# Wider splits, one evacuation for two PSUM banks, and half-size cache chunks in a decode layer with GLA and dilated attention

## The chip, the cores and the metric

The kernel runs on one core of a Trainium2 chip. The metric is device time in microseconds (us) of one execution. In the profile PE is TensorE (matrix multiply), PEld its weight load, DVE VectorE, ACT ScalarE, POOL GpSimd, SP SyncE (which only issues DMAs here).

## What is computed

One layer of a hybrid decoder on 544 tokens, 512 of a new prompt and 32 sampled ones (8 sequences of 4 tokens) whose attention reads a cached window. The reference, cut to what matters here:

```python
def layer(x):                                    # x: 544 tokens x 2048
    h = rmsnorm(x)
    gq, gk, gv, gg, glr, aq, ak, av = split(h @ w_in)
    log_a = log_sigmoid(glr @ w_gk_up + b_gk) / 16
    gla_o = gla_chunked(gq, gk, gv, log_a, state)    # 4 heads, S_t = diag(a_t) S_{t-1} + k_t v_t
    # 8 heads, each query sees keys t - j*dil, j = 0..128, for dil = 1, 4, 16; sampled tokens read the cache
    att_o = combine([window_attention(aq, ak, av, cache, dil) for dil in (1, 4, 16)])
    y = concat(rmsnorm(gla_o) * silu(gg), rmsnorm(att_o))
    x = x + y @ w_out
    return x + square(relu(rmsnorm(x) @ w_up)) @ w_down
y = final_rmsnorm(layer(x))                      # also: new keys and values, GLA states
```

## The kernel before

Activations stand transposed, 128 features by 544 tokens a tile, and every large product is weights times such tiles in two column halves of 272. For precision each f32 factor is split into a high part (rounded to fp32r) and a low part (the remainder), and three products are summed: high by high, high by low, low by high.

The stages on TensorE, in order: the in-projection (`slot_main`, slots 6 to 95), the output projection (`wo`, slots 96 to 127), the MLP as units of 12 matmuls, a last block and the final norm. A slot is half of the contraction of one block of 128 output features: 8 weight tiles of 128x128, three products, two column halves, 48 matmuls. Two slots fill one pair of PSUM banks, one bank for each half of the tokens; `bank[0..3]` are two such pairs. The first 16 slots of `wo` (96 to 111) read the attention's output, the other 16 that of GLA.

Ahead of its slot, weights are loaded (`raw`, 512 KB) and split by `split_w`: ScalarE copies to the high part `wh`, VectorE subtracts to the low part `wl`. A slot's weights are split in two units of 128x512, each with one instruction for the high and one for the low part, in rings of four high and three low tiles, four units ahead (`AHEAD`). A block is evacuated by `evac_in`, `evac_att` and `evac_wo` (VectorE) with one instruction per bank, 128x272.

The attention and GLA run in the background of the in-projection: they are Python generators, and `bg`, called twice in a slot, steps them, so that their instructions are queued on each engine between those of the slots. The order on each engine is thus fixed when the program is built. `att_sample` is the attention of the sampled tokens: for each of two groups of four heads, key chunks and then value chunks are loaded by SyncE (`kvload`, `kv` tiles, a ring of `NKV`) and worked off by VectorE. A chunk holds `VE` positions of 320 columns each; a key position is one multiply-add (into two accumulators in turn), a value position one dot product; there are `NCH` key and `NCH` value chunks a group. One step of the generator is one chunk. `bg` steps `att_sample` under this condition, with a planner's clocks `clk` for each engine:

```python
while clk["V"] + 1000 < clk["P"] + TH_S and step(sgens):   # TH_S = 1000
    pass
```

and each call of a VectorE operation first lifts VectorE's clock to TensorE's (line 96 of the profile is this helper, which issues nearly every instruction):

```python
self.clk[self.key] = max(self.clk[self.key], self.clk["P"] - self.clk["lag"])
self.clk[self.key] += self.cost(name, a, k)
```

When the slots of the in-projection are through, `drain` steps what is left until the attention is finished, and only then `wo` is issued. Names in the rows: `kv` are cache chunks, `wh` and `wl` the parts of weights, `bank` PSUM, `b` any other tile, `ones` a matrix for sums over partitions, `AT`, `ktok`, `vtok`, `ST`, `dlS` tiles of GLA.

Of the kernel before, what the change touches and what calls it, by code (L numbers as in the profile page):

```python
# [16 lines left out]
HALF = 272  # L17
# [3 lines left out]
VE = 4  # L21
NCH = 32
NROW = 320
NKV = 3
# [20 lines left out]
NWH = 3  # L45
NWHI = 4
AHEAD = 4
NSLOT2 = 7
# [75 lines left out]
def _body(ctx, nc, tc, A):  # L124
# [6 lines left out]
    bank = [psum.tile([128, 512], F32, name=f"bank{i}") for i in range(8)]  # L131
    mbank = bank[:4]
# [14 lines left out]
    def alloc(dt=F32):  # L147
        cnt[0] += 1
        n = f"b{cnt[0]}"
        for free, p, tag, bufs in tiers:  # L150
            if free[0]:
                free[0] -= 1
                t = p.tile([128, NTOK], dt, name=n, tag=tag, bufs=bufs)
                home[id(t)] = (t, free)
                return t
        raise SystemExit(f"no slots at {slot[0]} {unit_no}")
# [70 lines left out]
    def low_parts():  # L227
        while todo:
            todo.pop(0)()

    def split_w(key, r, eng, lag=False):

        low_parts()
        h = whm[key] = pool.tile([128, 4, 128], R32, name="wh" + "_".join(map(str, key)), tag="wh", bufs=NWHI)
# [11 lines left out]
        if not lag:  # L246
            low_parts()

    def split_q(i, q):
        split_w((i, q), raws[i][:, 4 * q:4 * q + 4, :], V, True)  # L250
# [13 lines left out]

    def wops(i):
        return (lambda c: whm[i, c // 4][:, c % 4, :]), (lambda c: wlm[i, c // 4][:, c % 4, :])
# [158 lines left out]
    def evac_in(idx, pb):  # L425
        kind, h, _ = order[idx]
        t = alloc()
        sc = QSCALE if kind in ("q", "gq") else 1.0
        for hf in range(2):
            V.scalar_tensor_tensor(half(t, hf), pb[hf][:, :HALF], sc, half(r_bc, hf), op0=OP.mult, op1=OP.mult)  # L430
        B[kind, h] = t
        ready[kind, h] = slot[0]
        if kind in ("q", "k", "v"):
            j = "qkv".index(kind)
            S.activation(KVS[h // 4][:, j * 128 + (h % 4) * 32:j * 128 + (h % 4) * 32 + 32], t[:, SEQ:], AF.Copy)
        if kind in ("k", "v"):
            dst = A["kT" if kind == "k" else "vT"][h]
            defer(1, lambda: nc.sync.dma_start(dst, t))
# [551 lines left out]
    for c in range(14):  # L990
# [12 lines left out]
        if c == 13:  # L1003
            for k in range(c - 2, 16):
                xsquare(k)
            load()
# [5 lines left out]
    for n in range(3):  # L1012
        xmm(n, 14)
        xmm(n, 15)
        if n == 0:
            prep_to(2)
            V.tensor_add(ssA, ssA, ssB)
            rms_r(r_bc, [ssA], D, (b0, b1))
            rel(ssA, ssB, *sqt)
# [36 lines left out]
    def slot_main(i, pb, xs_, c0, first, last, evac=None, nbg=1, hs=(0, 1)):  # L1056
        begin()
        load_to(i + NRAW + 1)
        prep_to(uidx[i] + AHEAD)
        h, l = wops(i)  # L1060
        for q in range(2):
            clk["P"] = max(clk["P"], spl[i, q])
# [11 lines left out]
            if q == 0:  # L1074
                prep_to(uidx[i] + AHEAD + 1)
# [115 lines left out]
    def evac_att(nb):  # L1191
        def f(pb):
            for hf in range(2):
                V.tensor_add(half(xr[nb], hf), pb[hf][:, :HALF], half(xr[nb], hf))
        return f

    def evac_wo(nb):
        def f(pb):
            t = xr[nb]
            for hf in range(2):  # L1200
                V.tensor_add(half(t, hf), pb[hf][:, :HALF], half(t, hf))
# [57 lines left out]
    FIRST = uidx[len(W) - 1] + 2  # L1259
# [55 lines left out]
    def product(key, ops, k, blocks, ps, start, stop):  # L1315
        def mm_():
            n = len(blocks)
# [32 lines left out]
    ua = [bank[0], bank[1]]  # L1350
    ub, uc = [bank[2], bank[6]], [bank[3], bank[7]]
# [3 lines left out]
    def halfb(b):  # L1355
        return b[:, :HALF]
# [64 lines left out]
    def up_after(p, k):  # L1421
        a, b, c = ua[p % 2], ub[p % 2], uc[p % 2]
# [5 lines left out]
        def f():  # L1428
            if k == "P1":
# [73 lines left out]
    for p, k, q in useq:  # L1503
        bk, st_ = ubank[k]
        i = len(units)
        for quad_, kk in last_read.items():
            if kk == k:
                raw_last["u", p, *quad_] = i
        add_unit(Unit((k, p, q), up_prep(p, k, q),
                      product((k, p, q), XU, k, range(4 * q, 4 * q + 4), halfb(bk[p % 2]), st_ and q == 0,  # L1510
# [35 lines left out]
    def down_after(g, p, k):  # L1546
        ps = halfb(bank[4 * (p % 2) + dbank[k][0]])

        def f():
            if g == 0 and k == "P1":  # L1550
                acc[2 * p], acc[2 * p + 1] = alloc(), alloc()
# [48 lines left out]
    for g in range(7):  # L1600
        for p in range(8):
            for i in range(2):
                raw_seq.append((("d", g, p, i), A["wdn"][g, 2 * p + i]))
            for k in D_ORDER:
# [3 lines left out]
                if k == "P4":  # L1608
# [3 lines left out]
                         product((k, g, p), XD[g], k, range(4), halfb(bank[4 * (p % 2) + b_]), st_, True),  # L1612
# [46 lines left out]
    LB = [bank[i] for i in (0, 1, 2, 3)]  # L1659
# [71 lines left out]
    def split_last(key, r):  # L1731
# [6 lines left out]
        h = whm[key] = pool.tile([128, 4, 128], R32, name="wh" + "_".join(map(str, key)), tag="wh", bufs=NWHI)  # L1738
# [5 lines left out]
    for hf in range(2):  # L1744
        for nb in range(16):
            raw_seq.append((("l", hf, nb), A["wdn"][7, nb]))
            for q in range(2):
                raw_last["l", hf, nb] = len(units)

                def prep(hf=hf, nb=nb, q=q):  # L1750
                    split_last(("L", hf, nb, q), mraw["l", hf, nb][:, 4 * q:4 * q + 4, :])
                add_unit(Unit(("L", hf, nb, q), prep, last_mm(hf, nb, q), before=last_before(hf, nb, q),
                              after=(lambda hf=hf, nb=nb: evac_last(hf, nb, LB[nb % 4])) if q else None))
# [39 lines left out]
    assert not later  # L1793

# [165 lines left out]
```

## Time and profile before

| | |
|---|---|
| three runs | 2323.55, 2325.3, 2328.4 us, median 2325.3 |
| the profiled execution | 2323.29 us, of which the span of the trace is 2321.5 us |
| TensorE busy | 2277.4 us, 98% of the span |
| VectorE busy | 1963.5 us, 85% |
| ScalarE busy | 1115.3 us, 48% |
| GpSimd busy | 126.7 us, 5% |
| DMA | 473.43 MB, mean 204 GB/s |
| in-projection, output projection | to 730 us; 730 to 927 us |

A busy share is an average over the span. A row of a timeline gives the start, the duration, the engine, the line and the operation with what it writes and reads; several equal instructions in a row are one row with their count, and in brackets stands how long the engine was idle before it and what ended that.

### The profile page before, as it was taken

To read this page: it belongs to the slowest core of one execution; us is meant where nothing else is said; L and a number is where in the kernel's file an instruction comes from. 1 tells how busy PE (TensorE), PEld (TensorE's weight loads), DVE (VectorE), ACT (ScalarE), POOL (GpSimd) and SP (SyncE) were. 2 spreads that over 40 slices of the span, in tenths; PEclk is the share of its full clock that TensorE was granted. 3 is DMA by queue.
4 is the path that set the end of the run, shared out by engine and by line. 5 is a ranking of instruction groups with operands and counts; after the bars stand their busy time and mean duration, and the time that the engine had idled before them with its cause. 6 is when DMAs were issued, how large, how long until landed. Compare 5 with 4: busy or idle time off the path is not lost.

```text
span 2321.5 us, 47246 instructions
## 1 busy us (share of the span) xinstructions
PE 2277.4 (98%) x17960; PEld 2247.7 (97%) x17960; DVE 1963.5 (85%) x4343; ACT 1115.3 (48%) x2133; POOL 126.7 (5%) x182
## 2 busy tenths in 40 slices
PE   8999999999999999999999999999999999999997
PEld 8999999999989999999999999999999999999997
DVE  7888877889878987888888888887788888888995
ACT  5333343333345345666666666655444444444465
POOL 3000010000012630000000000000000000000000
PEclk9999999999999999999999999999999999999999
DMA  6777865645735974365566556667755664664564
GB/s 228 265 266 240 287 227 189 219 144 186 242 104 173 349 259 162 112 207 180 186 199 203 177 188 205 197 198 255 266 175 169 217 208 150 217 222 154 170 214 149
DMA packets 168191, 473.43 MB, mean 204 GB/s; under 512 B 20091, under 2 KB 29307, under 8 KB 167964
## 3 DMA queue, kind: packets, MB, share of 16 engines
q1 hardware_dynamic: 157340, 439.67, 56.7%
q0 software_dynamic: 9472, 29.63, 3.6%
q8 instruction: 141, 2.31, 0.4%
q10 hardware_dynamic: 1152, 1.11, 0.1%
q14 instruction: 86, 0.70, 0.1%
HBM read 393.07 MB, written 77.27 MB: 203 GB/s over the span
## 4 chain that ended last, share of the span: by engine, by line
PE 86%; DVE 7%; DMA 4%; ACT 2%; issue 1%; POOL 0%; SPq 0%; DVEq 0%; ACTq 0%
PE bank L96 86%; DVE b L96 5%; DMA b<-vs 2%; ACT b L96 1%; DVE wlP L96 1%; DMA b<-xT 1%; DMA b<-hs 1%; DVE wl L96 1%; ACT whP L96 0%; DMA b<-win 0%; DMA raw<-win 0%; DVE AT L96 0%; ACT wh L96 0%; DVE kv L96 0%; POOL b L96 0%
## 5 line engine op out<-in xcount | busy, mean ns | idle before, releaser
L96 PE MATMUL bank<-b,whP 128*128 128x272 f32 x6720 | 980.4, 288 | 7.5 <-ACT b L96 3.6
L96 PEld LDWEIGHTS bank<-b,whP 128*128 128x128 f32 x6720 | 895.5, 188 | 10.4 <-ACT whP L96 4.4
L96 PE MATMUL bank<-b,wlP 128*128 128x272 f32 x3360 | 561.0, 289 | 2.1 <-DVE wlP L96 2.1
L96 PE MATMUL bank<-b,wh 128*128 128x272 f32 x3904 | 529.9, 288 | 0.3 <-DVE b L96 0.3
L96 PEld LDWEIGHTS bank<-b,wh 128*128 128x128 f32 x3904 | 505.3, 188 | 0.5 <-DVE b L96 0.5
L96 PEld LDWEIGHTS bank<-b,wlP 128*128 128x128 f32 x3360 | 472.9, 188 | 6.6 <-DVE wlP L96 3.4
L96 ACT ACTIVATE whP<-b 128x512 fp32r<-128x512 f32 x480 | 299.3, 627 | 255.7 <-DVE b L96 198.4
L96 ACT ACTIVATE b<-b 128x544 fp32r<-128x544 f32 (+6 forms) x485 | 274.6, 572 | 277.3 <-DVE b L96 245.7
L96 DVE TENSOR_TENSOR wlP<-b,whP 128x512 fp32r<-128x512 f32 x480 | 328.9, 686 | 17.0 <-ACT whP L96 16.5
L96 DVE TENSOR_TENSOR b<-b,b 128x272 f32<-128x272 f32 (+8 forms) x574 | 274.7, 498 | 35.8 <-ACT b L96 31.6
L96 PE MATMUL bank<-b,wl 128*128 128x272 f32 x1952 | 297.8, 295 | 2.7 <-DVE wl L96 2.6
L96 PEld LDWEIGHTS bank<-b,wl 128*128 128x128 f32 x1952 | 261.6, 189 | 9.8 <-issue 4.4
L96 ACT ACTIVATE b<-bank 128x272 f32<-128x272 f32 (+4 forms) x247 | 98.0, 409 | 316.8 <-PE bank L96 293.4
L96 DVE TENSOR_TENSOR b<-b,bank 128x272 f32<-128x272 f32 x388 | 167.3, 433 | 58.4 <-PE bank L96 57.9
L96 DVE TENSOR_TENSOR wl<-raw,wh 128x512 fp32r<-128x512 f32 x244 | 167.0, 692 | 54.7 <-PE bank L96 30.9
L96 ACT ACTIVATE wh<-raw 128x512 fp32r<-128x512 f32 x244 | 149.4, 623 | 128.3 <-PE bank L96 116.0
L96 DVE TENSOR_TENSOR wlP<-mraw,whP 128x512 fp32r<-128x512 f32 x206 | 140.8, 687 | 47.5 <-ACT whP L96 39.1
L96 PE MATMUL bank<-b,b 128*128 128x272 f32 (+5 forms) x968 | 143.1, 304 | 6.3 <-ACT b L96 6.3
L96 ACT ACTIVATE whP<-mraw 128x512 fp32r<-128x512 f32 x206 | 124.0, 621 | 41.4 <-PE bank L96 40.6
L96 POOL TENSOR_TENSOR b<-b,b 128x544 f32<-128x544 f32 (+2 forms) x26 | 36.4, 1403 | 1885.7 <-ACT b L96 1773.3
L96 DVE TENSOR_TENSOR wlP<-raw,whP 128x512 fp32r<-128x512 f32 x154 | 105.4, 687 | 34.5 <-ACT whP L96 28.3
L96 PEld LDWEIGHTS bank<-b,b 128*128 128x128 f32 (+2 forms) x968 | 119.3, 180 | 12.3 <-ACT b L96 6.6
(92 smaller groups left out, 1668.5 us busy)
## 6 DMA issues: line engine op xcount, KB each, us to landing
hs<-b SPq DMA_DIRECT2D x196, 272.0 KB, 6.0
b<-hs SPq DMA_DIRECT2D x196, 272.0 KB, 4.9
raw<-win SPq DMA_DIRECT2D x90, 512.0 KB, 4.2
mraw<-wdn SPq DMA_DIRECT2D x82, 512.0 KB, 3.6
kv<-kcg SPq DMA_DIRECT2D x64, 640.0 KB, 5.3
kv<-vcg SPq DMA_DIRECT2D x64, 640.0 KB, 5.4
mraw<-wup SPq DMA_DIRECT2D x74, 512.0 KB, 4.1
raw<-wdn SPq DMA_DIRECT2D x62, 512.0 KB, 3.7
```

The lines of the kernel that those rows point to most:

```text
L96: return f(*a, **k)
```

## The change

Sizes. `VE` goes from 4 to 2 and `NCH` from 32 to 64, so a chunk has half the positions and there are twice as many; `NKV` goes from 3 to 5. Loads become 320 KB each in place of 640 KB, 128 and 128 of them in place of 64 and 64.

Splits. In the two projections a slot's weights are split as one unit of 128x1024, in a ring of two tiles each for high and low (`NW8`), and one unit ahead (`uidx[i] + 2`). The high part is issued at the start of the slot before, the low part in that slot's middle (`low_parts`). 122 + 122 instructions take the place of 244 + 244. The MLP takes halves of the same tiles (`w4`).

Evacuations. The two bank pairs become two tiles `duo` of 128x2x512; `both` reads the pair, and one instruction evacuates 2x272 columns: 46 of 128x544 and 4 of 128x272 in place of 96 in the in-projection, 32 in place of 64 in the output projection. The pool of `duo` is closed ahead of the MLP, whose banks 0 to 3 come from a new pool. `NSLOT2` goes from 7 to 5 (tiles for intermediate results that are spilled).

```diff
-VE = 4
-NCH = 32
+VE = 2
+NCH = 64
-NKV = 3
+NKV = 5
-NWH = 3
-NWHI = 4
-AHEAD = 4
-NSLOT2 = 7
+NW8 = 2
+NSLOT2 = 5
...
-    bank = [psum.tile([128, 512], F32, name=f"bank{i}") for i in range(8)]
-    mbank = bank[:4]
+    duo = [duo_pool.tile([128, 2, 512], F32, name=f"duo{i}") for i in range(2)]
+    mbank = [duo[i // 2][:, i % 2, :] for i in range(4)]
+    bank = mbank + [psum.tile([128, 512], F32, name=f"bank{i}") for i in range(4, 8)]
...
+    def split_i(i):
+
+        low_parts()
+        h = whm[i] = w8("wh", i)
         clk["lag"] = 1e9
-        S.activation(h, r, AF.Copy)
+        S.activation(h, raws[i], AF.Copy)
         clk["lag"] = 0.0
 
         def low():
-            l = wlm[key] = pool.tile([128, 4, 128], R32, name="wl" + "_".join(map(str, key)), tag="wl", bufs=NWH)
+            l = wlm[i] = w8("wl", i)
             clk["lag"] = 1e9
-            eng.tensor_sub(l, r, h.bitcast(F32))
+            V.tensor_sub(l, raws[i], h.bitcast(F32))
             clk["lag"] = 0.0
-            spl[key] = clk[eng.key]
+            spl[i] = clk["V"]
         todo.append(low)
...
-        for hf in range(2):
-            V.scalar_tensor_tensor(half(t, hf), pb[hf][:, :HALF], sc, half(r_bc, hf), op0=OP.mult, op1=OP.mult)
+        if any(pb[0] is m for m in mbank):
+            V.scalar_tensor_tensor(halves(t), both(pb), sc, halves(r_bc), op0=OP.mult, op1=OP.mult)
...
-        prep_to(uidx[i] + AHEAD)
+        prep_to(uidx[i] + 2)
...
             if q == 0:
-                prep_to(uidx[i] + AHEAD + 1)
+                low_parts()
+                if i == len(W) - 1:
+                    prep_to(uidx[i] + 3)
...
-                V.tensor_add(half(t, hf), pb[hf][:, :HALF], half(t, hf))
+            V.tensor_add(halves(t), both(pb), halves(t))
...
+    duoctx.close()
+    mlp_pool = ctx.enter_context(tc.tile_pool(name="ps3", bufs=1, space=bass.MemoryType.PSUM))
+    bank[:4] = [mlp_pool.tile([128, 512], F32, name=f"bank{i}") for i in range(4)]
```

How the order on the engines changes. First VectorE in the middle of the in-projection, around the splits of slots 15 and 16; `kv13` is the 13th chunk in either program, `b104` and `b105` are the two accumulators. Before:

```order
L96 TENSOR_TENSOR wl15_1_1308<-raw15_1063,wh15_1_1262 128x512
L96 SCALAR_TENSOR_TENSOR b104_822<-kv13_1229,b104_822 128x320
L96 SCALAR_TENSOR_TENSOR b105_825<-kv13_1229,b104_822,b105_825 128x320
L96 SCALAR_TENSOR_TENSOR b104_822<-kv13_1229,b104_822 128x320
L96 SCALAR_TENSOR_TENSOR b105_825<-kv13_1229,b104_822,b105_825 128x320
L96 TENSOR_TENSOR wl16_0_1344<-raw16_1164,wh16_0_1310 128x512
L96 SCALAR_TENSOR_TENSOR b104_822<-kv14_1280,b104_822 128x320
L96 SCALAR_TENSOR_TENSOR b105_825<-kv14_1280,b104_822,b105_825 128x320
L96 SCALAR_TENSOR_TENSOR b104_822<-kv14_1280,b104_822 128x320
L96 SCALAR_TENSOR_TENSOR b105_825<-kv14_1280,b104_822,b105_825 128x320
L96 TENSOR_TENSOR wl16_1_1378<-raw16_1164,wh16_1_1346 128x512
```

Now:

```order
L94 SCALAR_TENSOR_TENSOR b104_781<-kv13_1044,b104_781 128x320
L94 SCALAR_TENSOR_TENSOR b105_784<-kv13_1044,b104_781,b105_784 128x320
L94 TENSOR_TENSOR wl15_1248<-raw15_1024,wh15_1204 128x1024
L94 SCALAR_TENSOR_TENSOR b104_781<-kv14_1091,b104_781 128x320
L94 SCALAR_TENSOR_TENSOR b105_784<-kv14_1091,b104_781,b105_784 128x320
L94 SCALAR_TENSOR_TENSOR b104_781<-kv15_1137,b104_781 128x320
L94 SCALAR_TENSOR_TENSOR b105_784<-kv15_1137,b104_781,b105_784 128x320
L94 TENSOR_TENSOR wl16_1310<-raw16_1117,wh16_1280 128x1024
L94 SCALAR_TENSOR_TENSOR b104_781<-kv16_1176,b104_781 128x320
L94 SCALAR_TENSOR_TENSOR b105_784<-kv16_1176,b104_781,b105_784 128x320
L94 SCALAR_TENSOR_TENSOR b117_1340<-duo1_70,b37_160 128x544
```

A slot still has two chunks of the sampled attention, each now of two multiply-adds in place of four.

Second TensorE at the end of the in-projection. `wl95` is the low part of its last slot, `wh96` the high part of the first slot of the output projection, `b316` and (in the changed program) `b322` the first operand made from the attention's output. Before:

```order
L96 MATMUL bank0_66<-b94_527,wl95_1_8470 128x272
L96 MATMUL bank1_67<-b94_527,wl95_1_8470 128x272
L96 MATMUL bank2_68<-b316_8310,wh96_0_8472 128x272
L96 MATMUL bank3_69<-b316_8310,wh96_0_8472 128x272
L96 MATMUL bank2_68<-b317_8311,wh96_0_8472 128x272
```

Now the last matmul of slot 95 is followed by small ones of GLA's last head, of which the first four rows are shown,

```order
L94 MATMUL duo0_69<-b92_504,wl95_7595 128x272 x2
L94 MATMUL duo0_69<-b94_528,wl95_7595 128x272 x2
L94 MATMUL bank4_71<-b279_6480 128x128 x2
L94 MATMUL bank5_72<-b280_6485 128x128 x2
L94 MATMUL bank6_73<-b296_7667 128x128 x2
L94 MATMUL bank7_74<-b297_7672 128x128 x2
```

and these end with the sums and transposes of the attention:

```order
L94 MATMUL bank7_74<-b309_7906,ones_83 128x272
L94 MATMUL bank4_71<-b309_7906,ones_83 128x272
L94 MATMUL bank5_72<-cst_82,b313_8067 128x128 x4
L94 MATMUL bank6_73<-cst_82,b314_8068 128x128 x4
L94 MATMUL bank7_74<-cst_82,b284_6895 128x128
L94 MATMUL bank4_71<-b286_6903,ones_83 128x272
L94 MATMUL bank5_72<-b286_6903,ones_83 128x272
L94 MATMUL duo1_70<-b322_8388,wh96_7627 128x272 x2
```

In the rows before nothing stood between the two projections; now the rest of GLA's head 3, the end of the sampled attention and the norms do.

Third VectorE at the last value chunk, numbered 128 before and 256 now; `b168` and `b284` hold the result of the sampled attention. Before:

```order
L96 SCALAR_TENSOR_TENSOR kv127_7548,b168_3690<-kv127_7548,b168_3690 128x320 x4
L96 SCALAR_TENSOR_TENSOR b291_7665<-bank2_68,b37_159 128x272
L96 SCALAR_TENSOR_TENSOR b291_7665<-bank3_69,b37_159 128x272
L96 TENSOR_TENSOR wl87_0_7670<-raw87_7526,wh87_0_7635 128x512
L96 SCALAR_TENSOR_TENSOR kv128_7619,b168_3690<-kv128_7619,b168_3690 128x320 x4
L96 TENSOR_TENSOR wl87_1_7702<-raw87_7526,wh87_1_7672 128x512
L96 SCALAR_TENSOR_TENSOR b168_3690<-b230_5539,b168_3690 128x128 x4
```

Now:

```order
L94 SCALAR_TENSOR_TENSOR kv253_8321,b284_6895<-kv253_8321,b284_6895 128x320 x2
L94 SCALAR_TENSOR_TENSOR kv254_8325,b284_6895<-kv254_8325,b284_6895 128x320 x2
L94 SCALAR_TENSOR_TENSOR kv255_8329,b284_6895<-kv255_8329,b284_6895 128x320 x2
L94 SCALAR_TENSOR_TENSOR kv256_8333,b284_6895<-kv256_8333,b284_6895 128x320 x2
L94 SCALAR_TENSOR_TENSOR b284_6895<-b314_8068,b284_6895 128x128 x4
L94 TENSOR_SCALAR b319_8370<-bank4_71 128x272
```

Before, the last chunk stood ahead of the split for slot 87; now it stands behind the split for slot 96, with no split or evacuation between the last chunks, and the first chunk behind that split is `kv150`:

```order
L94 TENSOR_TENSOR wl96_7686<-raw96_7499,wh96_7627 128x1024
L94 SCALAR_TENSOR_TENSOR b298_7712<-duo0_69,b37_160 128x544
L94 SCALAR_TENSOR_TENSOR b284_6895<-kv150_7549,b284_6895 128x320
L94 SCALAR_TENSOR_TENSOR b285_6898<-kv150_7549,b284_6895,b285_6898 128x320
L94 COPY_PREDICATED AT_80<-msk_84,bank4_71 128x2x64 x2
```

The evacuation of the in-projection's last block (`b298`, out of `duo0`) is now one instruction, and all chunks from 150 on come behind it.

## Rows read from the trace of the kernel before

**Rows 1.** The page's first part: busy us, share of the span and instructions by engine.

```profile
PE 2277.4 (98%) x17960; PEld 2247.7 (97%) x17960; DVE 1963.5 (85%) x4343; ACT 1115.3 (48%) x2133; POOL 126.7 (5%) x182
```

**Rows 2.** Table by stage: stretch, length, busy by engine, granted clock, DMA share, GB/s.

```profile
660.00:730.00 70.00, 62.10 (x477) 59.08 (x476) 54.54 (x135) 34.49 (x60) 11.38 (x15) 0.98 0.35 116
```

**Rows 3.** Timeline of TensorE at the seam: start, duration, engine, line, operation.

```profile
662.96 1.29 PE L96 MATMUL bank<-b,wh 128*128 128x272 f32 x9
...
720.75 2.18 PE L96 MATMUL bank<-b,ones 128*128 128x272 f32 x4 [3.34 <-DVE b L96]
722.34 1.93 PE L96 MATMUL bank<-b,wl 128*128 128x272 f32 x8
724.11 2.17 PE L96 MATMUL bank<-b,wh 128*128 128x272 f32 x16
...
729.12 1.17 PE L96 MATMUL bank<-b,wl 128*128 128x272 f32 x8
730.12 2.17 PE L96 MATMUL bank<-b,wh 128*128 128x272 f32 x16
```

**Rows 4.** Timeline of VectorE at the end of the sampled attention.

```profile
647.39 0.48 DVE L96 SCALAR_TENSOR_TENSOR kv<-kv,b 128x320 f32<-128x320 f32 x1
...
648.65 1.51 DVE L96 SCALAR_TENSOR_TENSOR b<-b,b 128x128 f32<-128x128 f32 x4
```

**Rows 5.** Timeline of VectorE, four operations of GLA's last head.

```profile
668.87 0.89 DVE L96 COPY_PREDICATED AT<-msk,bank 128x128 f32<-128x128 uint8 x4
...
685.91 0.69 DVE L96 COPY vtok<-bank 128x512 f32<-128x512 f32 x1 [1.70 <-PE bank L96]
...
691.55 0.28 DVE L96 TENSOR_TENSOR b<-bank,b 128x32 f32<-128x32 f32 x2 [3.43 <-ACT b L96]
...
704.47 0.78 DVE L96 SCALAR_TENSOR_TENSOR b<-b,nw,b 128x544 f32<-128x544 f32 x1
```

**Rows 6.** Timeline of VectorE in a key chunk and in a value chunk.

```profile
84.36 0.55 DVE L96 SCALAR_TENSOR_TENSOR b<-kv,b 128x320 f32<-128x320 f32 x1
84.82 0.55 DVE L96 SCALAR_TENSOR_TENSOR b<-kv,b,b 128x320 f32<-128x320 f32 x1
...
242.40 0.49 DVE L96 SCALAR_TENSOR_TENSOR kv<-kv,b 128x320 f32<-128x320 f32 x1
...
243.23 0.49 DVE L96 SCALAR_TENSOR_TENSOR kv<-kv,b 128x320 f32<-128x320 f32 x1
```

**Rows 7.** Timeline of VectorE between a group's keys and values.

```profile
465.18 0.49 DVE L96 TENSOR_TENSOR b<-b,b 128x320 f32<-128x320 f32 x1
...
483.81 0.29 DVE L96 SCALAR_TENSOR_TENSOR b<-b,b 128x128 f32<-128x128 f32 x1 [0.31 <-ACT b L96]
```

**Rows 8.** Table by stage, a stretch in which the DMA engines were wholly busy.

```profile
75.00:80.00 5.00, 5.00 (x42) 5.00 (x42) 4.15 (x9) 1.27 (x2) 0.00 (x0) 1.00 1.00 385
```

**Rows 9.** Timeline of GpSimd, the last addition of the attention's squares.

```profile
687.64 1.69 POOL L96 TENSOR_TENSOR b<-b,b 128x544 f32<-128x544 f32 x1 [2.21 <-ACT b L96]
```

**Rows 10.** Timeline of VectorE: two heads of the attention's output, and a reciprocal root.

```profile
714.39 0.78 DVE L96 SCALAR_TENSOR_TENSOR b<-b,nw,b 128x544 f32<-128x544 f32 x1
...
716.54 0.78 DVE L96 SCALAR_TENSOR_TENSOR b<-b,nw,b 128x544 f32<-128x544 f32 x1
...
725.50 0.43 DVE L96 TENSOR_SCALAR b<-bank 128x272 f32<-128x272 f32 x1
...
727.97 0.92 DVE L96 SCALAR_TENSOR_TENSOR b<-b,b 128x272 f32<-128x272 f32 x2
```

**Rows 11.** Groups by line and form: busy us, mean ns, idle before and its releasers.

```profile
L96 DVE TENSOR_TENSOR wl<-raw,wh 128x512 fp32r<-128x512 f32 x244 | 167.0, 692 | 54.7 <-PE bank L96 30.9 <-ACT wh L96 17.0 <-ACT b L96 5.0
...
L96 DVE SCALAR_TENSOR_TENSOR b<-bank,b 128x272 f32<-128x272 f32 x96 | 37.5, 434 | 15.9 <-PE bank L96 15.7
```

**Rows 12.** Timeline of TensorE where the MLP begins.

```profile
932.34 2.15 PE L96 MATMUL bank<-b,whP 128*128 128x272 f32 x8 [3.59 <-ACT b L96]
```

**Rows 13.** View of one tile, `kv`: time from issue to landing of its loads.

```profile
DMA to landing us min/median/max: 3.8/5.3/7.9
```

More of the change, by code (lines that the diff above doesn't have):

```diff
@@ L155, in alloc @@
                 return t
-        raise SystemExit(f"no slots at {slot[0]} {unit_no}")
+        raise SystemExit(f"no slots at {slot[0]} {[x for x in B]} {len(AO)}")
     def rel(*ts):
@@ L263, in half, with halves, both @@
         return t[:, hf * HALF:(hf + 1) * HALF]
+    def halves(t):
+        return t.rearrange("p (a n) -> p a n", a=2)
+    def both(pb):
+        return duo[0 if pb[0] is mbank[0] else 1][:, :, :HALF]
     def wops(i):
-        return (lambda c: whm[i, c // 4][:, c % 4, :]), (lambda c: wlm[i, c // 4][:, c % 4, :])
+        return (lambda c: whm[i][:, c, :]), (lambda c: wlm[i][:, c, :])
     def mm(pb, w, x, start, stop, hs=(0, 1)):
@@ L428, in evac_in @@
         sc = QSCALE if kind in ("q", "gq") else 1.0
-        for hf in range(2):
-            V.scalar_tensor_tensor(half(t, hf), pb[hf][:, :HALF], sc, half(r_bc, hf), op0=OP.mult, op1=OP.mult)
+        if any(pb[0] is m for m in mbank):
+            V.scalar_tensor_tensor(halves(t), both(pb), sc, halves(r_bc), op0=OP.mult, op1=OP.mult)
+        else:
+            for hf in range(2):
+                V.scalar_tensor_tensor(half(t, hf), pb[hf][:, :HALF], sc, half(r_bc, hf), op0=OP.mult, op1=OP.mult)
         B[kind, h] = t
@@ L1005, in _body @@
                 xsquare(k)
-            load()
+            load_to(6 + NRAW)
         for n in range(3):
@@ L1192, in f @@
         def f(pb):
-            for hf in range(2):
-                V.tensor_add(half(xr[nb], hf), pb[hf][:, :HALF], half(xr[nb], hf))
+            V.tensor_add(halves(xr[nb]), both(pb), halves(xr[nb]))
         return f
@@ L1199, in f @@
             t = xr[nb]
-            for hf in range(2):
-                V.tensor_add(half(t, hf), pb[hf][:, :HALF], half(t, hf))
+            V.tensor_add(halves(t), both(pb), halves(t))
             sq = {}
@@ L1313, in add_unit, with product @@
         preps.append(prep)
-    def product(key, ops, k, blocks, ps, start, stop):
+    def product(key, ops, k, blocks, bk, start, stop):
         def mm_():
+            ps = halfb(bank[bk])
             n = len(blocks)
@@ L1509, in _body @@
         add_unit(Unit((k, p, q), up_prep(p, k, q),
-                      product((k, p, q), XU, k, range(4 * q, 4 * q + 4), halfb(bk[p % 2]), st_ and q == 0,
+                      product((k, p, q), XU, k, range(4 * q, 4 * q + 4), bk[p % 2], st_ and q == 0,
                               q == 1),
@@ L1611, in _body @@
                 u = Unit((k, g, p), down_prep(g, p, k),
-                         product((k, g, p), XD[g], k, range(4), halfb(bank[4 * (p % 2) + b_]), st_, True),
+                         product((k, g, p), XD[g], k, range(4), 4 * (p % 2) + b_, st_, True),
                          after=down_after(g, p, k))
@@ L1737, in split_last @@
             return split_w(key, r, V)
-        h = whm[key] = pool.tile([128, 4, 128], R32, name="wh" + "_".join(map(str, key)), tag="wh", bufs=NWHI)
+        h = whm[key] = w4("wh")
         l = wlm[key] = kept_lo[nb, q][:, :512].rearrange("p (c n) -> p c n", c=4)
@@ L1752, in _body @@
                 add_unit(Unit(("L", hf, nb, q), prep, last_mm(hf, nb, q), before=last_before(hf, nb, q),
-                              after=(lambda hf=hf, nb=nb: evac_last(hf, nb, LB[nb % 4])) if q else None))
+                              after=(lambda hf=hf, nb=nb: evac_last(hf, nb, bank[nb % 4])) if q else None))
     xr_load(nbs[0])
```

41 lines of the change are left out of this document (25 added, 16 removed).

## The prediction

> **What bounds the kernel now.** I read the busy line first [rows 1]: TensorE works 2277.4 of 2321.5 us (98%), VectorE 1963.5 (85%). So time can only be won in TensorE's 44 us of idle time, and any wait of TensorE is paid in full. Next the table by stage around the seam between the two projections [rows 2]: from 660 to 730 TensorE is busy 62.1 of 70 us at a mean granted clock of 0.98 of full, and that is where the change's two ends meet. Then TensorE's timeline there [rows 3]. An undisturbed slot of the in-projection (48 large matmuls) takes 724.11 to 730.12, 6.01 us. The six slots before it, from 662.96 to 724.11, take 61.15 us where six would take 36.1: 25.0 us are small matmuls of the last GLA head and of the attention's norm, and waits for VectorE (one of 3.34 us). The output projection follows at 730.12 without a gap. That it can is due to VectorE's timeline [rows 4]: the last dot product of the sampled attention starts at 647.39, the last four multiply-adds of its result at 648.65, some 80 us before the operand made from them is due. Everything below hangs on that lead.
>
> **Part 1, the smaller chunks: the lead goes.** In the code one background call steps the sampled attention once and hardly ever twice: the step's own vector calls lift the planner's vector clock to TensorE's, and its loop asks that this clock lie behind. There are 90 slots with two calls each. 128 chunks and a dozen other steps fit into 180 calls; 256 chunks do not. The order of the changed program bears this out: behind the last matmul of the in-projection and ahead of the first of the output projection stand 43 key chunks (numbers 150 to 192), all 64 value chunks of the second group (193 to 256), the rest of GLA head 3 and the attention's norm. All of the first 16 slots of the output projection read the attention's output, so TensorE has nothing else queued: the work, formerly beside matmuls, stands on the path. Costs, in order of the chain:
>
> (a) *Gain first.* The 25.0 us of the last slots, small matmuls and waits, leave the in-projection. I let it end at 730.1 - 25.0 = 705 us.
> (b) *GLA head 3.* Between 668.87 and 704.47 [rows 5] lie VectorE's operations of this head; without splits, evacuations and the attention's heads they sum to about 23.5 us, the first being 0.89 and the last 0.78 us. The waits inside were filled by splits before and now are bare: 1.70 and 3.43 us on two of the rows, with the shorter ones about 7.4. In the order 12 key chunks stand among them. A chunk is two multiply-adds, and these start 0.463 us apart [rows 6] (84.36 and 84.82): 0.93 a chunk, 11.1 in all. Sum 42.0 us.
> (c) *The other 31 key chunks*, 0.93 each and a little for the wait on the load: 0.95 x 31 = 29.5 us.
> (d) *Between keys and values*: the sum and eight copies (1.5 us from 465.18), transposes and two copies out of PSUM (1.9, an estimate), four dots and the maximum (2.2 from 483.81) [rows 7], exponential and scaling (1.1, an estimate by like widths): 6.7 us.
> (e) *64 value chunks.* Two dots start 0.83 us apart over a chunk's worth (242.40 to 243.23, two steps) [rows 6], so VectorE needs 0.82 to 0.83. A chunk is 327,680 bytes, and where the DMA engines were wholly busy they moved 385 GB/s [rows 8], 0.85 us a chunk. The later of the two holds: 0.85 x 64 = 54.4 us. The Trainium skill (DMA: Bandwidth & Descriptors, "Where 436 GB/s comes from") gives a limit near 358 GB/s for transfers out of HBM; by it a chunk would take 0.92 us (an estimate) and the sum be 4 us larger, but the row's 385 lies above that limit, so I do not take it.
> (f) *The end chain*, each waiting for the one before: four multiply-adds 1.5 (648.65), transposes and copies 1.2 and a square 0.65 (estimates by [rows 7]), four GpSimd adds of up to 1.69 [rows 9] of which I count 6.0, the sums over partitions 0.8, the reciprocal root (3.4 from 725.50 to the end of the row at 727.97) [rows 10] with a hop 4.3, scaling and first head 1.5 (two operations of some 0.75): 16.0 us.
>
> The gap is 42.0 + 29.5 + 6.7 + 54.4 + 16.0 = 148.6 us. Its bounds: 135 if the waits of (b) vanish and GpSimd's adds overlap the dots; 180 if half of the chunks wait for loads at the pace of the first rival.
> (g) *Heads.* The first output slot then gets its eight operands as VectorE and ScalarE make them, one per 2.15 us (714.39 to 716.54) [rows 10]: 17.2 where a slot takes 6.0, +11.
> (h) *Clock.* After the wait of 3.34 us eight matmuls took 1.93 us where eight take 1.17 at 729.12 [rows 3]: TensorE came out of an idle at the lower level of its clock (1.2 GHz) and lost 0.8 us on these eight. I count the restart behind the gap and one more place: +2.
>
> **Part 2, wide splits and evacuations.** A split's subtraction of 128x512 takes 692 ns and a 128x272 evacuation 434 [rows 11], a slope of 1.075 ns a column. So 1024 columns cost 1.24 where two halves cost 1.38: 0.14 us x 122 = 17 us of VectorE; 544 columns cost 0.73 for 0.87: 0.14 x 78 = 11 us; ScalarE saves likewise. Worth nothing by itself: these lie beside matmuls, and VectorE has 15% free. What they give back is at most the short waits of TensorE left in slots 6 to 88, some 3 us. The price is lead: a unit was split four halves ahead, and now one whole unit ahead in a ring of two, its low part issued behind a background step. As VectorE loses half of the sampled attention's work there (two of four operations a call), it is less behind than before, and I count 0, with -3 to +8 as the bounds. A wide evacuation frees both banks together, with a second pair for the next block: 0.
>
> **Part 3, the rest.** The MLP's first unit now waits for the last evacuation, since its banks come from a new pool. TensorE waits there already, 3.59 us at 932.34 [rows 12]; +-1 us. Two fewer spill slots bunch some reloads between the MLP's halves: 0 to +2. The same matmuls run in the MLP, in the same order: 0. The doubled number of chunk loads costs SyncE issue time alone; it has nothing else to do.
>
> **Rivals.**
> *A, the gap is paced by loads.* Landing of a chunk took 5.3 us at the median at double the size [rows 13]. Five buffers leave four loads in flight: if the halves land no sooner, 5.3/4 = 1.33 us a chunk, over the 95 chunks of (c) and (e) 126 in place of 84 us, +42: 2504 us. For it: fixed cost may dominate and V already asks for the full 385 GB/s. Against: 3.8 us was seen at 640 KB, little else is loaded in the gap, and half the bytes should land faster. The Trainium skill ("Measured (HBM→SBUF, 128 partitions, SWDGE, issued from GpSimd)" on the same page) says to batch transfers to at least 1 MiB; it speaks for this rival, though no row here has a load of 320 KB.
> *B, the short lead stalls the in-projection.* GLA has steps with several microseconds of VectorE work between background calls; a low part behind one comes late. With some 15 such steps at 2 us each, +30: about 2492. It decides if a low part lands over 2 us into its slot (behind the 16 matmuls that need only the high part). Against: lighter VectorE in that stage.
> *C, the other side: the chunks stay hidden.* If TensorE had matmuls to run beside the 107 chunks, or the background steps caught up twice a call as TensorE's clock ran on, only waits would go: the 7.9 us idle of 660 to 730 [rows 2] and some 3 elsewhere, about 2314. It decides whether anything stands on TensorE between the last in-projection matmul and the first that reads the attention's result. The order shows only the small matmuls of GLA and of the norms, so this nearly falls.
>
> **How the numbers follow.** Against the profiled run (2323.3 us): -25 + 148.6 + 11 + 2 = +136.6, 2460; the median of the runs shown, 2325.3, is 2 higher than that run, so **2462 us**. Chances: this forecast 0.70, A 0.15, B 0.10, C 0.02, other slowdowns 0.03. Its own range is 2436 to 2475. The low end: 14 from the gap's low bound, 6 if half of the head term overlaps, 3 from part 2, 3 from clock and seam. The range reaches over B to A with 4 more for the other bounds: 2436 to 2508. Measurement can tell about 0.2% here (5 us); every case but C lies far over it: slower 0.97, same 0.01, faster 0.02.
>
> **What would show it.** In the changed profile TensorE should be busy to about 705 us, then hold one gap of near 150 us with a few small matmuls in it, and restart near 853 us with a first output slot of about 17 us; TensorE's busy sum stays near 2277 us and the MLP keeps its length. VectorE in the last 55 us of value chunks should be packed at 0.85 us a chunk. Step (e) falls if VectorE waits for loads there (A); part 2 falls if TensorE waits for low parts before 700 us (B); the whole falls if the output projection starts near 730 us (C).

## The result, and the profile after

The changed kernel took 2468.53 us (median of 4 runs, 2466.75 to 2468.91), the one before 2325.07 us beside it: 1.0607 times, 95% interval 1.0592 to 1.0622. The forecast was 2462 us, range 2436 to 2508. The profiled execution took 2468.6 us, its span is 2466.8 us, 145.3 more than the 2321.5 of before.

The page's first two parts, busy time by engine and three lines of the 40 slices, answer to [rows 1]:

```profile
PE 2295.0 (93%) x17960; PEld 2260.9 (92%) x17960; DVE 1949.4 (79%) x4144; ACT 1091.3 (44%) x2011; POOL 126.1 (5%) x182
...
PE   8999999999960099999999999999999999999997
...
PEclk9999999999985589999999999999999999999999
DMA  6555543444548769435566665556856546655564
```

TensorE was 98% busy and is 93%: the hole is three slices wide, and in it the granted clock falls to half. The table by stage (stretch, length, busy time of PE, PEld, DVE, ACT and POOL, granted clock, DMA share, GB/s) shows the seam, for [rows 2]; while VectorE works off bare chunks the DMA engines are 0.87 (keys) to 0.91 (values) busy:

```profile
660.00:700.20 40.20, 40.20 (x323) 40.20 (x322) 27.54 (x58) 11.60 (x15) 0.00 (x0) 1.00 0.57 195
700.20:745.00 44.80, 19.82 (x113) 16.24 (x112) 40.27 (x115) 11.97 (x22) 0.00 (x0) 0.69 0.46 140
...
739.10:772.20 33.10, 0.00 (x0) 0.00 (x0) 29.49 (x63) 0.00 (x0) 0.00 (x0) 0.50 0.87 285
...
778.30:844.90 66.60, 0.00 (x0) 0.00 (x0) 55.25 (x256) 0.00 (x0) 0.00 (x0) 0.50 0.91 304
845.00:860.60 15.60, 2.66 (x5) 1.35 (x5) 5.44 (x13) 5.09 (x13) 11.87 (x16) 0.50 0.36 106
860.60:885.80 25.20, 21.27 (x97) 17.82 (x98) 16.24 (x23) 9.66 (x15) 2.13 (x4) 0.67 0.30 99
885.80:1068.40 182.60, 182.06 (x1441) 180.62 (x1439) 152.08 (x260) 79.06 (x122) 67.92 (x127) 1.00 0.72 262
```

From 660 us to its end at 700.2 the in-projection now runs without an idle moment; then come 160 us in which TensorE has only small matmuls or nothing; from 885.8 on it is full again. Its timeline there answers to [rows 3], and the last row to [rows 12]:

```profile
699.16 1.17 PE L94 MATMUL duo<-b,wl 128*128 128x272 f32 x8
700.16 1.06 PE L94 MATMUL bank<-b 128*128 128x128 f32 x8
...
772.98 1.94 PE L94 MATMUL bank<-cst,b 128*128 128x128 f32 x8 [40.77 <-DVE b L94]
846.47 0.48 PE L94 MATMUL bank<-cst,b 128*128 128x128 f32 x1 [71.55 <-DVE b L94]
853.74 2.18 PE L94 MATMUL bank<-b,ones 128*128 128x272 f32 x4 [6.79 <-POOL b L94]
860.63 1.58 PE L94 MATMUL duo<-b,wh 128*128 128x272 f32 x4 [4.72 <-ACT b L94]
862.78 1.58 PE L94 MATMUL duo<-b,wh 128*128 128x272 f32 x4 [0.56 <-ACT b L94]
...
868.44 2.02 PE L94 MATMUL duo<-b,wl 128*128 128x272 f32 x8
...
1070.07 1.25 PE L94 MATMUL bank<-b,whu 128*128 128x272 f32 x8 [1.58 <-DVE b L94]
```

Two long waits for VectorE (40.77 and 71.55 us), then one for GpSimd's additions, then one for the first head; the first heads then come 2.15 us apart (860.63, 862.78). VectorE's own timeline, one row at each seam of the prediction's chain, for [rows 4, 6, 7]:

```profile
739.12 0.55 DVE L94 SCALAR_TENSOR_TENSOR b<-kv,b 128x320 f32<-128x320 f32 x1
...
772.20 0.49 DVE L94 TENSOR_TENSOR b<-b,b 128x320 f32<-128x320 f32 x1
...
778.33 0.49 DVE L94 SCALAR_TENSOR_TENSOR kv<-kv,b 128x320 f32<-128x320 f32 x1
...
785.02 0.49 DVE L94 SCALAR_TENSOR_TENSOR kv<-kv,b 128x320 f32<-128x320 f32 x1 [0.82 <-DMA kv<-vcg]
...
844.90 1.51 DVE L94 SCALAR_TENSOR_TENSOR b<-b,b 128x128 f32<-128x128 f32 x4
```

The 31 bare key chunks lie between the first two rows (33.1 us), the step to the values up to the third (6.1), the 64 value chunks from there to the last (66.6). In [rows 6] dots followed each other; here some wait for a load, and the view of the tile `kv` sums it (idle us before a use and how often), with the landing time that answers to [rows 13]:

```profile
  DMA kv<-vcg: 11.2, 22
  ACT b L94: 5.6, 2
  DMA kv<-kcg: 3.5, 6
...
DMA to landing us min/median/max: 2.7/4.2/6.7
```

Of the wide instructions the groups by form (busy us, mean ns, idle before them) answer to [rows 11]:

```profile
L94 DVE TENSOR_TENSOR wl<-raw,wh 128x1024 fp32r<-128x1024 f32 x122 | 150.7, 1235 | 56.1 <-ACT wh L94 56.1
...
L94 DVE SCALAR_TENSOR_TENSOR b<-duo,b 128x544 f32<-128x544 f32 x46 | 33.1, 722 | 80.2 <-PE duo L94 80.0
```

1235 and 722 ns, where the slope of two rows had given 1.24 and 0.73 us.

### The profile page after: what moved, and what is told of

It reads as the page before. It is cut to its first block, busy times and chain, and to the rows that moved or that the text cites. A ratio compares the mean times of both kernels' runs of the same rounds, so it can differ in the third digit from the quotient of the medians.

```text
span 2466.8 us, 46744 instructions
## 1 busy us (share of the span) xinstructions
PE 2295.0 (93%) x17960; PEld 2260.9 (92%) x17960; DVE 1949.4 (79%) x4144; ACT 1091.3 (44%) x2011; POOL 126.1 (5%) x182
## 4 chain that ended last, share of the span: by engine, by line
PE 82%; DVE 7%; DMA 7%; issue 2%; ACT 2%; POOL 0%; SPq 0%; DVEq 0%; ACTq 0%; POOLq 0%
PE bank L94 57%; PE duo L94 25%; DVE b L94 5%; DMA b<-vs 2%; DMA kv<-vcg 2%; ACT b L94 1%; DMA kv<-kcg 1%; DVE wlu L94 1%; DVE kv L94 1%; DMA hs<-b 1%; DMA b<-hs 1%; DMA b<-xT 0%; DVE wl L94 0%; ACT whu L94 0%; POOL b L94 0%
## 5 line engine op out<-in xcount | busy, mean ns | idle before, releaser
L94 PE MATMUL bank<-b,whu 128*128 128x272 f32 x7232 | 1057.5, 288 | 8.1 <-DVE b L94 2.9
L94 PEld LDWEIGHTS bank<-b,whu 128*128 128x128 f32 x7232 | 964.9, 188 | 11.9 <-ACT whu L94 5.6
L94 PE MATMUL bank<-b,wlu 128*128 128x272 f32 x3368 | 563.2, 289 | 2.0 <-DVE wlu L94 2.0
L94 PE MATMUL duo<-b,wh 128*128 128x272 f32 x3840 | 528.6, 290 | 8.6 <-ACT b L94 8.1
L94 PEld LDWEIGHTS duo<-b,wh 128*128 128x128 f32 x3840 | 500.8, 189 | 12.9 <-ACT b L94 10.6
L94 PEld LDWEIGHTS bank<-b,wlu 128*128 128x128 f32 x3368 | 474.9, 188 | 6.7 <-DVE wlu L94 3.4
L94 ACT ACTIVATE whu<-b 128x512 fp32r<-128x512 f32 x480 | 296.3, 625 | 234.1 <-PE bank L94 131.4
L94 DVE TENSOR_TENSOR wlu<-b,whu 128x512 fp32r<-128x512 f32 x480 | 329.4, 687 | 28.7 <-ACT whu L94 27.5
L94 DVE TENSOR_TENSOR b<-b,b 128x272 f32<-128x272 f32 (+10 forms) x574 | 275.4, 499 | 56.2 <-ACT b L94 52.1
L94 PE MATMUL duo<-b,wl 128*128 128x272 f32 x1920 | 293.2, 295 | 0.9 <-DVE wl L94 0.9
L94 DVE TENSOR_TENSOR wl<-raw,wh 128x1024 fp32r<-128x1024 f32 x122 | 150.7, 1235 | 56.1 <-ACT wh L94 56.1
```

What stands on the lines that cost most here:

```text
L94: return f(*a, **k)
```

## The experiments

The theory is that the pace of the sampled attention is the loss: one chunk a background step, so halving the chunk halves the pace. Rivals: the small loads themselves, the short lead of the wide splits, and the wide evacuations. Each run stands with its edit against the kernel named.

**small_only: the chunks without the rest.** Against before:

```diff
-VE = 4
-NCH = 32
+VE = 2
+NCH = 64
-NKV = 3
+NKV = 5
```

> The kernel before with nothing but the smaller chunks (2 positions, 64 chunks a phase, five buffers); splits and evacuations stay narrow. Theory (the chunks' pace is the whole loss, the wide instructions are worth little): the same gap between the projections, some 150 to 160 us, and 2455 to 2475 us. Rival (the wide splits with their short lead carry a part of the loss): clearly under 2450 us. Rival (the wide splits pay and hide a larger loss): over 2480 us.

One run: 2472.29 us. The in-projection ends at 699.2 us and the output projection starts at 863.4. The smaller chunks alone bring the whole loss and the same gap (164.2 us, against 160.5). With them in place the rest of the change takes at most some 4 us off (2468.5 against 2472.3); the latter is one run, and runs of one kernel lie up to 13 us apart here, so this is not shown.

**two_a_step: the pace restored.** Against the changed kernel, in both loops over chunks:

```diff
-                yield
+                if c % 2:
+                    yield
```

> The changed kernel with two small chunks in each background step, so that the positions per step are those of before; loads stay at 320 KB. Theory (what costs is the pace and not the size of the loads): no gap, the last value chunk before slot 87, 2316 to 2332 us. Rival (small loads are themselves slower and keep VectorE and so TensorE waiting in the in-projection): over 2340 us.

2338.5 us, 1.0056 times before (1.0042 to 1.0069). The gap is gone: in the order no small matmul is left between the two projections, and the output projection starts right behind the in-projection, at 741.8 us. But the time lies between the two theories: 130 of 143 us come back, 12 or 13 do not. The profile places them: the in-projection is 10.4 us longer than before's, and what follows the output projection 3.8. The two in-projections, before and two_a_step, by the table by stage:

```profile
46.20:730.10 683.90, 671.36 (x5274) 652.39 (x5273) 562.82 (x1720) 248.05 (x530) 35.32 (x31) 1.00 0.62 211
```

```profile
47.50:741.80 694.30, 676.02 (x5274) 656.57 (x5273) 551.57 (x1584) 235.60 (x438) 33.32 (x31) 0.99 0.61 207
```

Of the 10.4 us, 4.7 are longer busy time of TensorE (676.0 against 671.4, at a mean granted clock of 0.99 against 1.00) and 5.7 are waits. The next runs seek their cause.

**small_two: small loads at the old pace.** The kernel before with both edits above.

> The kernel before with the smaller chunks (five buffers), two of them in each background step, so the positions per step are as before; splits, rings and evacuations as before. It has two_a_step's loads without its splits and evacuations. Theory (loads of 320 KB cost nothing while VectorE's pace is kept): within 0.2% of before, 2322 to 2330 us. Rival (the small loads are what two_a_step lost): 2335 us or more.

2327.17 us, 1.0001 times (0.9992 to 1.0011). Loads of 320 KB cost nothing that these runs resolve (0.1%) as long as VectorE works off as many positions a step. Their landing time was 4.1 us at the median, against 5.3 in [rows 13]. What two_a_step still loses is thus not the loads.

**ahead3: a shorter lead.** Against before:

```diff
-AHEAD = 4
+AHEAD = 3
```

> The kernel before with its narrow splits made three half-slot units ahead in place of four (one constant); tiles and rings as before. The first half of the next slot is then split at the slot's start and the second in its middle. Theory (the lead is what the wide splits lost at full pace): +4 to +12 us, 2330 to 2338 us, with TensorE waiting for wh and wl. Rival (the lead has room to spare): within 0.2% of before.

2334.26 us, 1.0033 times (1.0021 to 1.0046). One constant less of lead costs some 8 us (5 to 11 by the interval). The groups by form show it in the idle time of TensorE ahead of the matmuls that read `wl`, here for before, ahead3 and two_a_step, one row from each kernel's view:

```profile
L96 PE MATMUL bank<-b,wl 128*128 128x272 f32 x1952 | 297.8, 295 | 2.7 <-DVE wl L96 2.6
```

```profile
L96 PE MATMUL bank<-b,wl 128*128 128x272 f32 x1952 | 298.7, 295 | 11.8 <-DVE wl L96 11.8
```

```profile
L94 PE MATMUL duo<-b,wh 128*128 128x272 f32 x3840 | 523.4, 289 | 2.4 <-ACT wh L94 2.4
L94 PE MATMUL duo<-b,wl 128*128 128x272 f32 x1920 | 293.8, 295 | 5.6 <-DVE wl L94 5.6
```

2.6 us of waiting for the low part in before, 11.8 in ahead3; 8.0 for both parts in two_a_step. The places differ: 8.0 of ahead3's 11.8 us lie in the output projection, 6.4 of two_a_step's 8.0 in the in-projection. So ahead3 shows that a shorter lead costs, not that it is all that two_a_step lost. In the changed kernel, with its half pace and lighter VectorE, the wait for the low part is 0.9 us, and none for the high part shows:

```profile
L94 PE MATMUL duo<-b,wl 128*128 128x272 f32 x1920 | 293.2, 295 | 0.9 <-DVE wl L94 0.9
```

**narrow_split: narrow instructions, short lead.** Against two_a_step, the split of 1024 columns is made as two of 512 in the same place and tiles:

```diff
-        S.activation(h, raws[i], AF.Copy)
+        for z in (0, 4):
+            S.activation(h[:, z:z + 4], raws[i][:, z:z + 4, :], AF.Copy)
...
-            V.tensor_sub(l, raws[i], h.bitcast(F32))
+            for z in (0, 4):
+                V.tensor_sub(l[:, z:z + 4], raws[i][:, z:z + 4, :], h[:, z:z + 4].bitcast(F32))
```

> As two_a_step, with every split again as two instructions of 512 columns for the high part and two for the low, but in the same tiles, ring of two and places as the wide ones. Theory (the loss of two_a_step is the lead of one unit in a ring of two, and the width is worth little): 2334 to 2343 us, near two_a_step. Rival (the width of the instruction is the loss, since nothing can start before all 1024 columns are done): back to 2325 to 2330 us.

2338.73 us, 1.0052 times before (1.0038 to 1.0065): the same as two_a_step. The width is worth nothing that these runs resolve (0.1 to 0.2%). That leaves the lead, or the ring of two, as what the wide splits lose; the waits for splits in two_a_step and ahead3 point to it, but no run gave the wide splits more lead at the full pace, so it is argued and not shown.

**low_early: a try to lengthen the lead.** Against two_a_step, in `slot_main`:

```diff
         prep_to(uidx[i] + 2)
+        low_parts()
```

> As two_a_step (two small chunks a background step, 2338.5 us, in-projection 694.3 us against 683.9 before), but the low part of the next slot's weights is issued at the slot's start, right after the high part and ahead of the background steps, not in the slot's middle. Theory (the short lead of the wide split is what the in-projection lost, TensorE waiting for wl and wh): the in-projection shortens by 4 to 9 us, 2329 to 2334 us. Rival (the place does not matter, VectorE simply has no room, or it now waits for ScalarE instead): 2337 us or more.

2395.26 us, 1.0297 times (1.0283 to 1.0311): by its time the rival's side, but not for the rival's reason. The edit moved more than the split: 22 value chunks and GLA's last head were left for the drain. That the step loop saw other planner clocks and took fewer steps is the likely way, not looked at. The table by stage shows a gap again:

```profile
727.80:789.00 61.20, 25.87 (x120) 19.33 (x118) 49.98 (x191) 18.31 (x36) 12.37 (x16) 0.64 0.48 154
```

It says nothing on the lead. It shows a second time that what is left over at the end of the in-projection is paid at full price.

**evac_only and narrow_evac: the evacuations alone.** evac_only puts the wide evacuations, with their bank pairs and the new pool of the MLP, into the kernel before; narrow_evac takes only the wide instructions out of two_a_step:

```diff
-            V.tensor_add(halves(t), both(pb), halves(t))
+            for hf in range(2):
+                V.tensor_add(half(t, hf), pb[hf][:, :HALF], half(t, hf))
```

(and so for the other two evacuations).

> The kernel before with the wide evacuations alone (the two bank pairs as duo tiles, one instruction a block, the MLP's banks from a new pool); splits, rings and chunks as before. Theory (the 11 us of VectorE saved lie beside matmuls): within 0.2% of before, 2321 to 2328 us. Rival (wide evacuations free a pair of banks later, or the new pool holds up the MLP): 2330 us or more.

2332.79 us, 1.0023 times (1.0014 to 1.0032): the rival's side, by a little.

> As two_a_step, with the evacuations again one instruction a bank. Theory: +0 to +4 us against two_a_step's 2338.5 (VectorE does 11 us more), so 2338 to 2343 us. Rival (the wide evacuation is what costs the 12 us of two_a_step): 2326 to 2330 us.

2335.2 us, 1.0038 times (1.0025 to 1.0052), between the two theories, and 3 to 4 us less than two_a_step, though the two intervals overlap. Both point the same way: wide evacuations do not gain at full pace; with the new pool they cost some 5 us (3 to 7 by evac_only's interval). Of evac_only's part one place is seen, where the MLP begins. In [rows 12] its first unit ran before the wait; now that unit waits for the last evacuation, since its banks come from a new pool:

```profile
936.11 1.25 PE L96 MATMUL bank<-b,whP 128*128 128x272 f32 x4 [5.38 <-DVE b L96]
```

That is 1.8 us more than the 3.6 of before. Its in-projection is 3.6 us longer. Up to 673.5 us two waits that before lacks stand in small matmuls of the attention and of GLA, 1.52 us for ScalarE at 327.21 and 1.12 for VectorE at 418.29; over the rest TensorE's granted clock was 0.92, where before had 0.97. Why wide evacuations would bring this stays open.

**nslot2_5: fewer spill tiles.** Against before, `NSLOT2 = 5` in place of 7.

> The kernel before with five in place of seven extra tiles for spilled intermediate results (NSLOT2), nothing else. The MLP took 4 us longer in the changed kernel. Theory (these tiles are the cause): +2 to +5 us, 2328 to 2332 us. Rival (the cause is elsewhere): within 2 us of before.

2331.14 us, 1.002 times (1.0004 to 1.0035): slower by 1 to 8 us, as the theory had it. TensorE's timeline between the MLP's halves shows three waits for reloaded tiles, where before has one (0.97 us at 1625.15):

```profile
1626.31 0.39 PE L96 MATMUL bank<-b,whP 128*128 128x272 f32 x1 [0.23 <-DMA b<-hs]
1627.68 0.39 PE L96 MATMUL bank<-b,whP 128*128 128x272 f32 x1 [0.98 <-DMA b<-hs]
1629.05 1.13 PE L96 MATMUL bank<-b,whP 128*128 128x272 f32 x5 [0.97 <-DMA b<-hs]
```

The changed kernel has the same three (0.44, 0.98, 0.96 us from 1765.76 on). The waits by themselves are about 1.2 us more, but the clock falls with them. In 12 us from where the waits begin, nslot2_5 and then before:

```profile
1625.30:1637.30 12.00, 9.81 (x61) 9.05 (x60) 7.95 (x14) 4.68 (x10) 0.00 (x0) 0.86 0.97 378
```

```profile
1623.50:1635.50 12.00, 11.03 (x86) 10.66 (x85) 10.50 (x18) 6.44 (x13) 0.00 (x0) 1.00 0.93 334
```

At a granted clock of 0.86 in place of 1.00 TensorE gets through 61 matmuls in place of 86. At 0.126 us each (eight take 1.0 us at the full clock) the missing 25 are 3.1 us, an estimate from these rows: most of the median's difference of 5. The changed kernel has 61 in the 12 us from 1764.6, two_a_step 63 in those from 1633.0.

**half_dots and ring3: what paces the gap.** half_dots leaves out one of the two dots of each value chunk of the second group, and keeps all loads; ring3 is the changed kernel with three buffers:

```diff
-                for e in range(VE):
+                for e in range(VE - g):
                     n = c * VE + e
                     dot(t[:, e * NROW:(e + 1) * NROW], sc[:, :NROW], oc[:, n:n + 1])
```

> The changed kernel with one of the two dot products of each value chunk of the second group left out (its output columns are not computed); all loads stay. VectorE then needs 0.41 us a chunk in place of 0.83. In the changed kernel the 64 chunks took 66.9 us. Theory (the loads pace the gap): the 64 chunks still take 58 to 67 us and the time is 2458 to 2468 us. Rival (VectorE paces it, with the waits an addition to its own work): they take some 40 us and the time is about 2442 us.

One run: 2464.18 us. The 64 value chunks take 63.0 us in place of 66.6 (by the rows above; the expectation has 66.9), though VectorE does half the work.

```diff
-NKV = 5
+NKV = 3
```

> The changed kernel with three chunk buffers in place of five, so two loads in flight in place of four. Theory A (in the gap the DMA engines' throughput limits, the number in flight does not): the 95 chunks stay near 1.05 us, 2466 to 2475 us. Theory B (landing time over loads in flight limits): with a landing time between the least seen, 2.7 us, and the median, 4.2 us, 1.35 to 2.1 us a chunk, +28 to +100 us, so 2496 us or more.

One run: 2505.09 us, and the 64 chunks take 91.8 us. The value chunks in the tables by stage, half_dots and then ring3, beside 304 GB/s at a share of 0.91 in the changed kernel:

```profile
775.80:838.80 63.00, 0.00 (x0) 0.00 (x0) 31.16 (x127) 0.00 (x0) 0.00 (x0) 0.50 0.94 319
```

```profile
789.10:880.90 91.80, 0.00 (x0) 0.00 (x0) 57.64 (x257) 0.00 (x0) 0.00 (x0) 0.50 0.75 226
```

So the loads pace the gap: VectorE is busy half of the time in half_dots and the phase hardly shortens. While VectorE works on a chunk, four loads are in flight in the changed kernel and in half_dots, and the DMA engines are 0.91 to 0.94 busy; in ring3 two are, and the engines are 0.75 busy. The view of `kv` over the gap alone, from 745 to 845 us in the changed kernel and from 755 to 881 in ring3:

```profile
DMA to landing us min/median/max: 2.9/4.1/5.3
```

```profile
DMA to landing us min/median/max: 2.7/3.3/4.1
```

Divided by the pace (1.04 and 1.43 us a chunk) the medians give 3.9 and 2.3 loads in flight on average, an estimate.

What no run tests is the size of the loads here, where they are not hidden. The 385 GB/s of [rows 8] came while loads of 512 and 640 KB were on the way, 4096 and 5120 bytes a partition; a load in the gap has 2560. The 304 GB/s at a share of 0.91 is 334 for engines wholly busy (an estimate), still under 385.

**lead5: the freed memory spent on lead.** Against small_two: `NKV = 4`, `NWH = 4`, `NWHI = 5`, `AHEAD = 5`, `NSLOT2 = 5`.

> What the memory of smaller chunks could be spent on: small_two with four chunk buffers, five high and four low split tiles and the splits five half-slot units ahead, NSLOT2 5. Theory (before has little to gain, since TensorE hardly waits for splits there; and NSLOT2 costs its share): 2324 to 2332 us. Rival (more lead takes waits out of the in-projection): below 2321 us, faster than both kernels.

2331.03 us, 1.0017 times (1.0008 to 1.0027). TensorE no longer waits for any low part (0.0 us, by the same group as above), and yet the kernel is no faster: before had only 2.6 us of such waits to give. Its output projection is 4.1 us shorter than before's, what follows 5.8 us longer (it has nslot2_5's fewer spill tiles), and the in-projection 7.1 us longer: 3.9 us of longer busy time (granted clock 0.99 for 1.00) and one wait of 3.32 us for VectorE, at 259.99, that before lacks; the cause of both was not sought. None of the runs beats the kernel before.

## Why the prediction was right

The mechanism held, shown by small_only (it alone brings the gap), small_two (the same loads at the old pace bring none) and two_a_step. Term by term, against the profiled execution:

| step | forecast us | measured us |
|---|---|---|
| (a) end of the in-projection | 705 | 700.2 |
| (b) GLA's last head with 12 key chunks | 42.0 | 37.9 (701.2 to 739.1) |
| (c) 31 key chunks | 29.5 | 33.1 |
| (d) keys to values | 6.7 | 6.1 |
| (e) 64 value chunks | 54.4 | 66.6 |
| (f) end chain | 16.0 | 15.7 |
| the gap as a whole | 148.6 | 160.5 |
| (g) first output slot | +11 | +12.1 |
| (h) clock | +2 | +0.9 in the second output slot, the rest within (g) |
| rest of the output projection | 0 | -2.2 |
| seam and MLP | 0 to +3 | +4.0 |

The sum came within 9 us of the measured 145.3, in part by luck: 16 us too little in one term stood against 9 us of errors the other way, 5 in (a) and 4 in (b). **(e), with (c), was 16 us too small**: the price of a chunk was taken from the highest rate that a row showed, 385 GB/s over 5 us [rows 8], where the gap sustained 304 at a DMA share of 0.91. Keys and values both ran at 1.04 to 1.07 us a chunk, though VectorE alone needs 0.93 and 0.83; half_dots shows that the load is the pacer. So by the prediction's own sign step (e) fell: VectorE was to be packed at 0.85 us a chunk, and it waited for loads 22 times there, 11.2 us. Rival A's mechanism is there, at 1.05 us and not at 1.33: the landing time of half the bytes was 4.2 us and not 5.3, and 4.2 over four in flight is 1.05. **(a) gained 5 us more**: the slots 6 to 88 lost 109.0 us over their 6.02 each where they had lost 117.1, against a start 3.2 us later; I had allowed 3 us. VectorE was lighter there; small_only, with narrow splits and evacuations, ends its in-projection at 699.2 us, so the smaller chunks bring this gain. The waits inside (b) were smaller than counted (VectorE was idle 4.5 us there, and 7.4 were counted), since key chunks fill them.

The bound of 385 GB/s was taken from one row of 5 us, and the gap did not hold it. The Trainium skill's limit near 358 GB/s for HBM (DMA: Bandwidth & Descriptors, "Where 436 GB/s comes from") makes 0.92 us a chunk, an estimate: nearer to the measured 1.05 than my 0.85, and still below it; the row of 385 lies above that limit. Another rule on that page of the Trainium skill, to batch transfers to at least 1 MiB, spoke for rival A. small_two shows that halving the loads costs nothing while they are hidden, and in the gap the number in flight moved the rate (ring3).

**Part 2 at 0** was right for this kernel and for the wrong reason in part. The wide instructions saved what the slope said (1235 and 722 ns). Rival B, the short lead, is real at the full pace: two_a_step shows 8.0 us of waits for splits where before has 2.6, and ahead3 costs 0.33%. Here it was hidden (0.9 us), with VectorE's chunk work halved in that stage by the same change; I named this cover, and two_a_step shows what comes without it. That wide evacuations with their new pool cost some 5 us at full pace I had put at 0; evac_only shows the step wrong, though small_only leaves no such loss in the changed kernel.

**Rival C** fell: the output projection started at 860.6 us. Two more signs given for the profile after failed. TensorE's busy sum did not stay at 2277 but rose by 17.6 to 2295 us: by 9.0 in the output projection, whose first two slots ran in part at a granted clock of 0.50, by 5.2 in the in-projection and the gap, by 3.4 behind them. And the MLP did not keep its length: with the seam it took 4.0 us more, some 3 of them at the three waits for spilled tiles (nslot2_5).

## What to carry to other kernels

Before halving the size of a piece of background work, look at what sets how many pieces are taken: where a schedule takes one a step, a smaller piece is a slower pace, and the rest is paid without cover at the next join. Count the pieces left at that join in the order, and price them by the slowest of the engine, the landing time over the loads in flight, and a transfer rate taken from loads of the same shape over as long a stretch. A wider instruction saves its overhead only on an engine that someone waits for; the lead that its coarser tiles take away can cost more (at the full pace two_a_step lost 12 to 13 us, part of them in waits for splits).

## What the runs showed of the hardware

- The same 320 KB loads ran at 304 GB/s with four in flight and at 226 with two (DMA shares 0.91 and 0.75); the 385 GB/s of [rows 8] stood over 5 us only, and with larger loads.
- TensorE's granted clock was 0.50 (1.2 GHz) from 735 us through the idle stretch to 870.2 in the first output slot. There eight matmuls on low parts took 2.02 us for the usual 1.17. Behind matmuls that followed each other closely (867.06 to 871.05) it was 1.00 (2.4 GHz) from 871.3 to 873.5, where TensorE was idle for half of the time; then it was 0.50 again to 880.0, and 1.00 from 881.7 on, with matmuls back to back. In the gap it was at 1.00 too, from 720 to 730 us, while GLA's small matmuls came close together:

```profile
720.00:730.00 10.00, 5.82 (x38) 5.00 (x38) 8.72 (x31) 2.88 (x7) 0.00 (x0) 1.00 0.43 123
735.00:845.00 110.00, 1.94 (x8) 1.57 (x8) 93.15 (x349) 3.84 (x7) 0.00 (x0) 0.50 0.85 280
...
860.60:870.20 9.60, 7.88 (x24) 5.88 (x25) 6.69 (x10) 2.63 (x4) 0.00 (x0) 0.50 0.38 146
871.30:873.50 2.20, 1.04 (x5) 0.60 (x5) 1.45 (x3) 0.66 (x1) 0.00 (x0) 1.00 0.00 0
874.20:880.00 5.80, 5.18 (x20) 4.61 (x21) 3.57 (x5) 4.84 (x8) 0.00 (x0) 0.50 0.19 52
881.70:885.70 4.00, 4.00 (x34) 4.00 (x33) 1.79 (x3) 0.78 (x1) 2.13 (x4) 1.00 0.39 73
```

- Short waits can cost more than they last: three waits of 0.23 to 0.98 us in nslot2_5, 1.2 us more waiting than in before, came with a granted clock of 0.86 over 12 us and some 3 us lost.
